# The feed-forward runs of an encoder trunk: the last columns first, then five seven-product groups on a tree of bank copies

## The chip, the core and the metric

The kernel runs on one core of a Trainium2 chip. The metric is the device time of one execution in microseconds (us). The kernel before takes 909.61 us, the median of two timed runs (909.1 and 910.12). Five engines work side by side: TensorE (PE, with PEld its weight loads), VectorE (DVE), ScalarE (ACT), GpSimd (POOL) and SyncE (SP), which issues loads.

## The reference

Two layers; x is 256 tokens of 1024 numbers in float32, and the inner width FF is 2816.

```python
def swiglu(h, w_gate, w_up, w_down):
    return (jax.nn.silu(h @ w_gate) * (h @ w_up)) @ w_down

for l in range(DEPTH):                      # DEPTH = 2
    x = x + 0.5 * swiglu(rms_norm(x, ffn1_norm[l]), ffn1_w_gate[l], ffn1_w_up[l], ffn1_w_down[l])
    h = rms_norm(x, mix_norm[l])
    ...                                     # h @ w_in, windowed and differential attention
    x = x + jnp.concatenate([out_a, out_b], axis=-1) @ w_out[l]
    x = x + 0.5 * swiglu(rms_norm(x, ffn2_norm[l]), ffn2_w_gate[l], ffn2_w_up[l], ffn2_w_down[l])
return rms_norm(x, final_norm)
```

## The kernel before

There are four feed-forward runs, called F1 to F4: layer 0's first (F1) and second (F2), layer 1's first (F3) and second (F4). Between F1 and F2, and between F3 and F4, stand the attention stages; F3 follows F2 directly.

**Precision.** Each weight is loaded as float32 into one of six raw buffers (`N_RAW`), by SP's queue. It is then split in two halves of 128x1024: ScalarE casts the high part (`CAST w<-raw`), VectorE takes the rest as the low part (`TENSOR_TENSOR w<-raw,w`). Activations are split in the same way (`CAST s<-ps`, `TENSOR_TENSOR s<-ps,s`). A product is then three matmuls: high by high, low by high, high by low. A product of a 128-token block with a 512x512 block of weights is 12 matmuls of 512 columns.

**Groups.** The inner width is five groups of 512 columns and a last piece of 256. Of a group, the gate and up weights are four blocks: a and d of the gate (upper and lower half of the 1024 inputs), b and c of the up weight. With two blocks of 128 tokens a group takes eight products of 12 matmuls. Most groups use seven products on sums of blocks, after Strassen and Winograd: sums of activations (`make_sums`, the q and v tiles) against sums of weights. In F1 groups 2 to 4 go by seven, in F2 to F4 groups 1 to 4; the others are plain. A sum of weights is made in a raw buffer, either by VectorE (`plus`, 128x2048) or by a load that POOL issues and that accumulates on arrival (`gather`). The results of several products are combined by accumulating in the same PSUM bank, by copies of banks on ScalarE and by additions on VectorE.

**From hidden to output.** The gated product (`silu` on ScalarE, `up` on VectorE) is turned by TensorE (`turn_one`: four transposes of 128x128; `turn` for the 256-column piece), split, and multiplied with the down weight, whose sums stay in PSUM over the run (`accs`). The last 256 columns (`gu`) come at the end of a run: their down product (`rest`, `tail`) follows group 4's first down product. Then `ffn_close` adds the result to x (`Residual.add`, `xk<-xk,ps`), and starts the next stage's norm: x is turned (`nxt.pair`), evicted with the gain and split, and its squares are summed.

**Order.** `Kept` (line 62 is where every instruction is issued, so all have one line in the profile) holds ScalarE, VectorE and POOL in the order of the program in the feed-forward runs; TensorE always. So an instruction that waits holds up all that stands behind it on its engine. The weights form one list of steps (`specs`). `ahead(n)` issues loads, sums (`prep`) and splits up to half step n. The tables in `LEAD` say, call by call of `go()`, how many half steps ahead of the current product that goes.

## Time and profile before

| | before |
|---|---|
| median of two runs | 909.61 us |
| span of the profiled execution | 907.5 us |
| PE busy | 899.1 us (99%) |
| DVE busy | 785.9 us (87%) |
| ACT busy | 609.8 us (67%) |
| POOL busy | 63.2 us (7%) |
| bytes by DMA | 200.83 MB, 221 GB/s |
| TensorE clock granted | 9 tenths or more in each of 40 slices |

The profiled execution has a span of 907.5 us; no total of its own is listed, and the timed runs' median is 2.1 us above its span, which is taken as what lies around a span. A row of the timeline reads: start, duration, engine, line, operation, output and inputs, count, and in brackets the idle time before it with what ended that. Neighbouring instructions of one form are one row with a count; other engines' rows lie in between. A row of the groups reads: busy time and mean ns of one, then idle time ahead and its releaser.

### The profile page before, as it was taken

The numbers are of one execution on the slowest core, as the hardware profiler recorded it, in microseconds if no ns is written. First come the engines' busy times: TensorE is split into PE (matmuls) and PEld (weight loads), VectorE is DVE, ScalarE is ACT, GpSimd is POOL, SyncE is SP. The second block draws the span as 40 slices with busy tenths as digits, with TensorE's granted clock in tenths as the row PEclk, the third lists the DMA queues.
The fourth block names the chain that finished last, engine by engine and source line by source line (L and its number), as shares of the span: only waits on it lengthen the run. The fifth ranks groups of instructions, "written<-read, shape, count | busy, mean of one in ns | idle before, by whom it ended". The sixth has DMA issues, their size and how long they took to land.

```text
span 907.5 us, 12030 instructions
## 1 busy us (share of the span) xinstructions
PE 899.1 (99%) x4468; PEld 751.0 (83%) x4468; DVE 785.9 (87%) x1069; ACT 609.8 (67%) x970; POOL 63.2 (7%) x79
## 2 busy tenths in 40 slices
PE   9999999999999999999999999999999999999997
PEld 7888888888888888888888888888888888888886
DVE  5968999879987899999778999988888978999894
ACT  6946677666776776677575776667667785776660
POOL 0401000000001001000000001000000000101011
PEclk9999999999999999999999999999999999999999
DMA  9998897954148798897976898899611786898731
GB/s 328 355 287 213 236 309 247 268 143 179 47 150 241 174 265 247 247 300 256 279 204 171 250 278 258 252 303 248 182 57 48 263 223 166 234 312 255 219 114 47
DMA packets 114331, 200.83 MB, mean 221 GB/s; under 512 B 3678, under 2 KB 31648, under 8 KB 114272
## 3 DMA queue, kind: packets, MB, share of 16 engines
q1 hardware_dynamic: 97616, 167.66, 54.4%
q0 software_dynamic: 16096, 31.75, 20.1%
q8 instruction: 35, 0.57, 0.2%
q10 hardware_dynamic: 560, 0.66, 0.2%
q14 instruction: 24, 0.20, 0.1%
HBM read 199.00 MB, written 1.05 MB: 220 GB/s over the span
## 4 chain that ended last, share of the span: by engine, by line
PE 98%; DMA 1%; issue 0%; SPq 0%; DVE 0%; POOLq 0%; POOL 0%
PE ps L62 73%; PE xy L62 25%; DMA xk<-in_x_dram 1%; SPq L172 0%; DVE s L62 0%; DVE xk L62 0%; POOLq L1285 0%; POOL rf L62 0%; SPq L469 0%; SPq L465 0%; DVE tot L62 0%; DVE tmp L62 0%
## 5 line engine op out<-in xcount | busy, mean ns | idle before, releaser
L62 DVE TENSOR_TENSOR w<-raw,w 128x1024 fp32r<-128x1024 f32 (+1 forms) x458 | 476.4, 1097 | 34.6 <-ACT w L62 33.2
L62 PE MATMUL ps<-w,s 128*128 128x512 f32 (+1 forms) x2046 | 473.6, 389 | 0.0
L62 PEld LDWEIGHTS ps<-w,s 128*128 128x128 f32 x2046 | 379.9, 188 | 78.7 <-issue 0.8
L62 ACT CAST w<-raw 128x1024 fp32r<-128x1024 f32 (+1 forms) x457 | 403.9, 954 | 54.0 <-DVE raw L62 38.7
L62 PE MATMUL xy<-w,s 128*128 128x512 f32 x528 | 125.8, 392 | 0.0
L62 PEld LDWEIGHTS xy<-w,s 128*128 128x128 f32 x528 | 98.2, 188 | 20.4
L62 PE MATMUL xy<-w,q 128*128 128x512 f32 x360 | 88.1, 393 | 0.0
L62 PEld LDWEIGHTS xy<-w,q 128*128 128x128 f32 x360 | 66.5, 188 | 13.3
L62 PE MATMUL ps<-s,w 128*128 128x512 f32 (+1 forms) x384 | 69.8, 338 | 0.0
L62 DVE TENSOR_TENSOR raw<-raw,raw 128x2048 f32<-128x2048 f32 x30 | 68.6, 2288 | 0.5
L62 POOL DMA_DIRECT2D raw<-in_ffn_w_up_dram x30 | 38.9, 1313 | 430.1 <-DVE w L62 264.9
L62 PEld LDWEIGHTS ps<-s,w 128*128 128x128 f32 x384 | 58.6, 188 | 8.5
L62 ACT ACTIVATE s<-ps,gcol 128x256 fp32r<-128x256 f32 (+1 forms) x80 | 31.4, 479 | 34.0 <-PE ps L62 34.0
L62 ACT CAST s<-ps 128x512 fp32r<-128x512 f32 x36 | 20.4, 592 | 43.2 <-PE ps L62 43.0
L62 PE MATMUL ps<-w,q 128*128 128x512 f32 x180 | 43.2, 389 | 0.0
L62 PE MATMUL ps<-w,v 128*128 128x512 f32 x180 | 43.2, 389 | 0.0
L62 DVE TENSOR_TENSOR s<-ps,s 128x512 fp32r<-128x512 f32 x36 | 24.1, 686 | 19.5 <-ACT s L62 19.3
L62 PEld LDWEIGHTS ps<-w,v 128*128 128x128 f32 x180 | 33.8, 188 | 7.0
L62 PEld LDWEIGHTS ps<-w,q 128*128 128x128 f32 x180 | 33.8, 188 | 7.0
L62 ACT ACTIVATE s<-s,negm 128x256 f32<-128x256 f32 x64 | 31.8, 498 | 5.3 <-DVE negm L62 5.3
L62 ACT COPY ps<-ps 128x512 f32<-128x512 f32 x15 | 8.6, 570 | 34.4 <-PE ps L62 34.4
L62 DVE SCALAR_TENSOR_TENSOR s<-ps,gcol,s 128x256 fp32r<-128x256 f32 x48 | 20.3, 477 | 13.0 <-ACT s L62 12.9
(131 smaller groups left out, 584.3 us busy)
## 6 DMA issues: line engine op xcount, KB each, us to landing
raw<-in_ffn_w_down_dram SPq DMA_DIRECT2D x44, 1024.0 KB, 7.0
raw<-in_ffn_w_gate_dram SPq DMA_DIRECT2D x39, 1024.0 KB, 7.7
raw<-in_ffn_w_up_dram SPq DMA_DIRECT2D x39, 1024.0 KB, 7.1
raw<-in_ffn_w_up_dram POOLq DMA_DIRECT2D x30, 1024.0 KB, 10.0
raw<-in_w_in_dram SPq DMA_DIRECT2D x14, 1024.0 KB, 6.7
raw<-in_ffn_w_gate_dram SPq DMA_DIRECT2D x8, 512.0 KB, 7.9
raw<-in_ffn_w_up_dram SPq DMA_DIRECT2D x8, 512.0 KB, 8.9
raw<-in_w_in_dram SPq DMA_DIRECT2D x8, 512.0 KB, 6.0
```

Source lines behind the costliest of these rows:

```text
L62: ins = issue(*a, **k)
```

## The change

In F2, F3 and F4 (`run`, `run_on`, `run_close` in place of the old loop):

- The last 256 columns come first: their first half (`g0`), then product a of group 0, then their second half (`g4`). Their hidden piece is turned after product d, and `rest` multiplies it at once. `rest` for the second half of the outputs comes in group 1.
- Group 0 also goes by seven, so all five groups do.
- The seven products accumulate in another order (`by_seven`): four banks A, B, Q, Y, where a is copied from A to Q, abc goes on in A and is copied to Y, and so on, with one copy more and one addition fewer.
- In group 0 (`WAYS`: "cd") both sums abc and abcd are made by accumulating loads of POOL. Block c is now loaded for itself (`load_also`).
- New tables of leads for each run, and another order of sums in `make_sums`, whose signs use `nhr`, the negated `hr`.
- At a run's end the down products of group 3 and 4 remain, with group 4's turn between; the residual of the second half is added by the next run (`late`, `late_sums`).

F1's groups 2 to 4 use the new `by_seven` too. In all, the list of instructions has 30 matmuls of 512 columns and 12 of 256 fewer, 18 weight splits and casts more, and 12 accumulating loads more (30 to 42).

**TensorE at the turn of the last 256 columns' hidden piece.** Before, at the end of F2: `s_807` is the hidden piece, `s_804` the turned halves of group 4, `ps_3058` and `ps_3225` banks of the output.

```order
L62 MATMUL ps_3059<-w_3997,s_804_4077 128x512 x2
L62 MATMUL ps_3059<-w_3998,s_804_4077 128x512
L62 MATMUL ps_4140<-ident,s_807_4108 128x128 x4
L62 MATMUL ps_3058<-w_3997,s_804_4077 128x512 x2
L62 MATMUL ps_3058<-w_3998,s_804_4077 128x512
L62 MATMUL ps_3059<-w_3997,s_804_4077 128x512 x2
L62 MATMUL ps_3059<-w_3998,s_804_4077 128x512
L62 MATMUL ps_3225<-w_4027,s_802_4069 128x512 x2
L62 MATMUL ps_3225<-w_4028,s_802_4069 128x512
L62 MATMUL ps_3226<-w_4027,s_802_4069 128x512 x2
L62 MATMUL ps_3226<-w_4028,s_802_4069 128x512
L62 MATMUL ps_3058<-w_4001,s_815_4145 128x512 x2
```

After, in F2's head: `xy_2806` is bank Q with the last matmuls of product d, `s_551` the hidden piece, `s_560` the same turned and split.

```order
L78 MATMUL xy_2806<-w_2743,s_527_2821 128x512
L78 MATMUL xy_2806<-w_2742,s_527_2821 128x512 x2
L78 MATMUL xy_2806<-w_2743,s_527_2821 128x512
L78 MATMUL ps_2874<-ident,s_551_2924 128x128 x4
L78 MATMUL ps_2983<-w_2835,s_560_2959 128x512 x2
L78 MATMUL ps_2983<-w_2836,s_560_2959 128x512
L78 MATMUL ps_2984<-w_2835,s_560_2959 128x512 x2
L78 MATMUL ps_2984<-w_2836,s_560_2959 128x512
```

The turn had twelve matmuls of other work behind it, six of them into `ps_3058` and six into `ps_3225`; now the turned piece is used by the matmul that follows.

**ScalarE at the same place.** Before: `tmp_4104` and `tmp_4106` are the silus of the last 256 columns, `s_815` the cast of the turned piece.

```order
L62 CAST s_802_4069<-ps_4064 128x2x256
L62 CAST s_804_4077<-ps_4072 128x2x256
L62 ACTIVATE tmp_4104<-xy_4021,r_2890 128x256
L62 ACTIVATE tmp_4106<-xy_4022,r_2890 128x256
L62 CAST w_4112<-raw_3929 128x1024
L62 CAST w_4116<-raw_3929 128x1024
L62 CAST s_815_4145<-ps_4140 128x2x256
L62 CAST w_4154<-raw_3969 128x1024
```

After: `tmp_2920` and `tmp_2922` are the silus of the last 256 columns, `tmp_2953` the silu of product d (`g0`), `s_560` the cast of the turned piece.

```order
L78 COPY xy_2806<-ps_2873 128x512
L78 CAST w_2914<-raw_2668 128x1024
L78 ACTIVATE tmp_2920<-ps_2790,r_2851 128x256
L78 ACTIVATE tmp_2922<-ps_2791,r_2851 128x256
L78 CAST w_2927<-raw_2670 128x1024
L78 CAST w_2931<-raw_2670 128x1024
L78 CAST w_2935<-raw_2003 128x1024
L78 ACTIVATE tmp_2953<-xy_2806,r_2851 128x512
L78 CAST s_560_2959<-ps_2874 128x2x256
L78 CAST w_2962<-raw_2003 128x1024
L78 CAST q_2970<-tmp_2967 128x4x128
```

Two weight casts stood between the silus and the cast of the turned piece; now three casts and a 512-column silu do. VectorE has its splits in the same order.

**VectorE at the head of F3.** Before: `xk` with `ps_3225` and `ps_3226` are the additions of the second half of the residual, ahead of the turn of x's second half.

```order
L62 TENSOR_TENSOR w_4215<-raw_4035,w_4214 128x1024
L62 SCALAR_TENSOR_TENSOR s_833_4229<-ps_4224,gcol,s_833_4229 128x256 x2
L62 SCALAR_TENSOR_TENSOR s_835_4239<-ps_4234,gcol,s_835_4239 128x256 x2
L62 TENSOR_TENSOR xk<-xk,ps_3225 128x512
L62 TENSOR_TENSOR xk<-xk,ps_3226 128x512
L62 TENSOR_TENSOR w_4267<-raw_4035,w_4266 128x1024
L62 SCALAR_TENSOR_TENSOR s_845_4299<-ps_4294,gcol,s_845_4299 128x256 x2
```

After, the same place: `ps_3121` and `ps_3122` are the banks of that half.

```order
L78 TENSOR_TENSOR w_4211<-raw_4049,w_4210 128x1024
L78 SCALAR_TENSOR_TENSOR s_819_4220<-ps_4215,gcol,s_819_4220 128x256 x2
L78 SCALAR_TENSOR_TENSOR s_821_4230<-ps_4225,gcol,s_821_4230 128x256 x2
L78 TENSOR_TENSOR w_4257<-raw_4044,w_4256 128x1024
L78 TENSOR_TENSOR xk<-xk,ps_3121 128x512
L78 TENSOR_TENSOR xk<-xk,ps_3122 128x512
L78 SCALAR_TENSOR_TENSOR s_833_4285<-xy_4279,gcol,s_833_4285 128x256 x2
L78 SCALAR_TENSOR_TENSOR s_834_4294<-xy_4280,gcol,s_834_4294 128x256 x2
```

A weight split (`w_4257`) now stands ahead of the two additions, where they had followed the low parts of the first half directly.

**ScalarE at the end of F2**, after the change only: `tmp_4079` is the silu of product abcd of group 4, `s_803` and `s_804` the casts of the turned hidden group 4.

```order
L78 ACTIVATE tmp_4079<-xy_2806,r_2851 128x512
L78 CAST w_4081<-raw_3856 128x1024
L78 CAST w_4086<-raw_3856 128x1024
L78 CAST w_4090<-raw_3977 128x1024
L78 CAST w_4094<-raw_3977 128x1024
L78 CAST w_4098<-raw_4010 128x1024
L78 CAST w_4124<-raw_4010 128x1024
L78 CAST s_803_4134<-ps_2874 128x512
L78 CAST s_804_4141<-xy_2807 128x512
```

Six weight casts stand between the silu and the first of the two casts.

The diff, cut to its core (`also`, `taker`, the old functions taken out and the unchanged parts are left out):

```diff
-SEVEN = ((2, 3, 4), (1, 2, 3, 4))
+SEVEN = (2, 3, 4)
+ORDER = (("g0", "a", "g4", "d", "ab", "rest", "bc", "abc", "c", "abcd"),
+         ("a", "d", "dn0", "ab", "abc", "bc", "c", "abcd"),
+         ("a", "dn1", "d", "dn0", "ab", "abc", "bc", "c", "abcd"))
+WAYS = ("cd", "", "", "", "")
...
+            head1=(2, 5, 10, 10, 10, 10, 10, 11, 14, 14, 14, 14, 15, 15, 15, 16, 16, 17, 21, 21, 22, 22, 22, 22, 22, 23),
+            end1=(6, 7, 12, 12, 13, 14),
...
+        parts = dict(a=Step(4, 512, load(a), key=a, free=[]),
+                     d=Step(4, 512, load(d), key=d, free=[]),
+                     ab=Step(4, 512, None, src=a, free=[], also=(c, w[c])),
+                     abc=Step(4, 512, None, prep=plus(c, a), src=a, free=[]),
+                     bc=Step(4, 512, load(b), key=b, added=True),
+                     c=Step(4, 512, None, src=c, added=False),
+                     abcd=Step(4, 512, None, prep=plus(d, a), src=a, free=[a, d], early=2))
+        steps = [parts[o] if isinstance(o, str) else o for o in order]
+        def begin():
+            if b in raws:
+                issue(gather(c, b), 1)
+            else:
+                parts["bc"].behind = gather(c, b)
+
+        steps[steps.index(parts["a"]) + 1].prep = lambda: issue(gather(b, a), 1)
+        steps[steps.index(parts["d"]) + 1].prep = begin
+        if "c" in ways:
+            parts["abc"].prep = None
+            steps[steps.index(parts["ab"]) + 1].prep = lambda: issue(gather(c, a), 1)
+        if "d" in ways:
+            parts["d"].free, parts["abcd"].free = [d], [a]
+            parts["abcd"].prep = None
+            steps[steps.index(parts["abc"]) + 1].prep = lambda: issue(gather(d, a), 1)
+        return steps
...
+        def run_specs(wg, wu, wd):
+            down = lambda g, h: plain(wd[l], h * 512, 512, 4 * g, 4)
+
+            def gu(k0):
+                def moves(t, ws=(wg[l], wu[l])):
+                    return [(t[:, :, h * 256:h * 256 + 256], rows(w, FF - 256, 256, k0, 4)) for h, w in enumerate(ws)]
+                return Step(4, 512, moves)
+
+            rest = plain(wd[l], 0, D, 4 * NGRP, 2)
+            for g in range(NGRP):
+                what = dict(g0=lambda: gu(0), g4=lambda: gu(4), rest=lambda: rest,
+                            dn1=lambda: down(g - 2, 1), dn0=lambda: down(g - 1, 0))
+                order = [what[o]() if o in what else o for o in ORDER[min(g, 2)]]
+                specs.extend(seven(wg[l], wu[l], g * 512, order, WAYS[g]))
+            specs.extend((down(NGRP - 2, 1), down(NGRP - 1, 0), down(NGRP - 1, 1)))
+
+        if l:
+            run_specs(g1, u1, d1)
...
+            s1 = add(b1, t1)
             high(s1)
             yield
-            low(0, v)
-            s2 = add(t0, s1, ALU.subtract)
-            low(1, s1)
-            b0_ = add(b0, s2, ALU.subtract)
-            yield
-            high(b0_)
+            s2 = less(s1, t0)
+            low(0, s1)
             high(s2)
             yield
-            low(2, b0_)
-            low(3, s2)
+            low(1, s2)
+            yield
+            v = add(t0, t1)
+            high(v)
+            yield
+            b0_ = less(s2, b0)
+            low(2, v)
+            high(b0_)
+            yield
+            low(3, b0_)
...
+        def late_sums(self, k, into=None):
+
+            if k == 1:
+                for j in range(2):
+                    self.nxt.pair(2 + j, into[j])
+            elif k == 2:
+                self.squares(1)
+                self.nxt.stats()
+                flush()
+
...
+        def by_seven(banks, take, go, then):
+
+            A, B, Q, Y = banks
+            prod(norm.quarter(0, 0), take("a"), A, True)
+            act.copy(Q, A)
+            then("a")
+            prod(norm.quarter(0, 1), take("d"), Q)
+            g0 = silu(flat(), Q, 0)
+            go()
+            then("d")
+            prod(norm.summed(1), take("abc"), A)
+            act.copy(Y, A)
+            go()
+            prod(norm.summed(0), take("ab"), B, True)
+            e = flat()
+            act.copy(e, B)
+            go()
+            then("abc")
+            prod(norm.summed(2), take("bc"), A)
+            act.copy(Q, A)
+            u1 = flat()
+            dve.tensor_tensor(u1, A, e, op=ALU.add)
+            go()
+            then("bc")
+            prod(norm.summed(3), take("c"), Y)
+            u0 = flat()
+            dve.tensor_tensor(u0, Y, e, op=ALU.add)
+            h = blk(F32)
+            up(h, u0, g0, 0, norm.nhr)
+            go()
+            prod(norm.quarter(1, 1), take("abcd"), Q)
+            g1 = silu(flat(), Q, 1)
+            go()
+            up(h, u1, g1, 1, norm.nhr)
+            return h
+
+        def run():
+
+            take = taker(ORDER[0])
+            caps, places = [iter(LEAD[t + str(which)]) for t in ("head", "aux")]
...
+            aux = counted()
+            go()
+            gu = [bank(), bank()]
+            w = take("g0")
+            tokens(gu, norm.xs, w, 0, (0, 1))
+            xy = pair()
+            norm.late(1, xy)
+            go()
+            tokens(gu, norm.xs, w, 0, (2, 3))
+            due(1)
+            hE, wr = [], []
+
+            def rest(h=0):
+                if not wr:
+                    wr.append(take("rest"))
+                accs.append([bank(), bank()])
+                tokens(accs[h], [None] * (2 * NGRP) + hE, wr[0], 4 * NGRP, range(2), first=4 * NGRP, last=-1, h=h)
+
+            banks = bank(), bank(), *xy
+
+            def then(what):
+                if what == "a":
+                    go()
+                    tokens(gu, norm.xs, take("g4"), 4)
+                    go()
+                    due(2)
+                    hE.append(hidden(gate([b[:, 0:256] for b in gu]), [b[:, 256:512] for b in gu]))
+                    go()
+                elif what == "d":
+                    hE[:] = turn(hE[0], 1, [banks[1]])
+                    go()
+                    rest()
+                    go()
+                    due(5)
+                elif what == "abc":
+                    due(7)
+                elif what == "bc":
+                    due(8)
+
+            return run_on(by_seven(banks, take, go, then), banks, rest)
+
+        def run_on(h, banks, rest, old=None, groups=range(1, NGRP)):
+            upto, more = [0], [None]
+
+            def go(table=None):
...
+            for g in groups:
+                go("next" if g == 1 else "last" if g == groups[-1] else "more")
+                new = []
+                take = taker(ORDER[min(g, 2)])
+                if aside is not None and rest is not None and g == groups[-1]:
+                    aside()
+
+                def then(what):
+                    if what == "a":
+                        if g > 1:
+                            add(old, g - 2, 1, take("dn1"))
+                        else:
+                            rest(1)
+                        go()
+                        new.append(turn_one(h, 0, banks[1]))
+                        go()
+                        new.append(turn_one(h, 1, banks[3]))
+                        go()
+                    elif what == "d":
+                        add(by_token(new), g - 1, 0, take("dn0"))
+                        go()
+
+                h = by_seven(banks, take, go, then)
+                old = by_token(new)
+            if rest is None:
+                return h, old
+            take = lambda: weights(99, True)
+            go("end")
+            w = take()
+            add(old, NGRP - 2, 1, w, range(3))
+            go()
+            new = by_token([turn_one(h, 0, banks[1]), turn_one(h, 1, banks[3])])
+            add(old, NGRP - 2, 1, w, range(3, 4), last=(-1, G4 - 1 if which == 2 * LAYERS - 1 else -1))
+            return accs, new, take, go
+
...
+    def run_close(parts, nxt):
+        accs, new, take, go = parts
+        res = Residual(nxt, accs)
+        go()
+        w = take()
+        tokens(accs[0], new, w, G4, first=-1, last=G4 + 3)
+        for t in range(2):
+            res.add(0, t)
+        go()
+        w = take()
+        tokens(accs[1], new, w, G4, (0, 1), first=-1, last=G4 + 3)
+        go()
+        for j in range(2):
+            nxt.pair(j)
+        nxt.copies(2)
+        res.squares(0)
+        tokens(accs[1], new, w, G4, (2, 3), first=-1, last=G4 + 3)
+        go()
+        for t in range(2):
+            res.add(1, t)
+        nxt.late = res.late_sums if nxt.sums else res.late
 
...
         nxt_norm.pair(0)
         out_part(w, 6, 1, [(0, 1)])
         nxt_norm.pair(1)
+        nxt_norm.copies(2)
+        res.squares(0)
         out_part(w, 6, 1, [(1, 1)])
-        res.squares(0)
         for t in range(2):
             res.add(1, t)
-        nxt_norm.late = res.late
+        nxt_norm.late = res.late_sums
```

324 lines of the change are left out of this document (151 added, 173 removed).

## The prediction

> **What bounds the kernel now.** I read the page's busy times and its chain of waits first, then the busy time by stage, then TensorE's own timeline.
>
> ```profile
> span 907.5 us, 12030 instructions
> PE 899.1 (99%) x4468; PEld 751.0 (83%) x4468; DVE 785.9 (87%) x1069; ACT 609.8 (67%) x970; POOL 63.2 (7%) x79
> PE 98%; DMA 1%; issue 0%; SPq 0%; DVE 0%; POOLq 0%; POOL 0%
> 277.69:306.19 28.50, 28.50 (x139) 23.81 (x138) 21.75 (x32) 21.76 (x41) 2.71 (x3) 1.00 0.84 222
> 337.04:367.85 30.81, 30.81 (x143) 25.60 (x141) 29.50 (x28) 21.90 (x27) 2.57 (x2) 1.00 0.90 257
> 425.97:452.30 26.33, 26.33 (x126) 21.89 (x125) 21.12 (x23) 17.09 (x21) 1.31 (x1) 1.00 0.93 284
> ```
>
> TensorE is busy 99% of the span and 98% of the chain of waits is TensorE itself: whatever else is done today is hidden. The three stretches (columns: length, then busy time of PE, PEld, DVE, ACT and POOL, the clock, the DMA share, GB/s) are the head of the second feed-forward run, its steady group 3, and its end. TensorE never waits in any of them. But in the steady group VectorE has only 30.81 − 29.50 = 1.31 us to spare; in the head 6.75, at the end 5.21. So two things count: how many matmuls go, and whether the work around the new places of use still comes in time. The later runs are called F2, F3, F4 here, as in the description of the kernel.
>
> ```profile
> 309.04 8.32 PE L62 MATMUL ps<-w,s 128*128 128x512 f32 x36
> 317.20 1.07 PE L62 MATMUL ps<-w,q 128*128 128x512 f32 x4
> L62 PE MATMUL ps<-w,s 128*128 128x256 f32 x36 | 4.5, 283 | 0.0
> ```
>
> The pace is (317.20 − 309.04)/36 = 0.2267 us for a 512-column matmul, so 2.72 for a product of 12, and 4.5/36 = 0.125 for 256 columns.
>
> **Part 1, the matmuls.** Group 0 goes from eight products to seven in three runs; the instruction lists hold 30 fewer 512-column matmuls and 12 fewer of 256. 30 × 0.2267 + 12 × 0.125 = 8.3 us less. All of TensorE's time is on the path, so this counts in full: **−8.3**.
>
> **Part 2, the hidden piece of the last 256 columns.** Before, it was turned at the end of the run:
>
> ```profile
> 441.85 0.60 PE L62 MATMUL ps<-ident,s 128*128 128x128 f32 x4
> 442.20 6.19 PE L62 MATMUL ps<-w,s 128*128 128x512 f32 x26
> 442.48 0.59 ACT L62 CAST s<-ps 128x512 fp32r<-128x512 f32 x1 [2.14 <-PE ps L62]
> 443.10 0.69 DVE L62 TENSOR_TENSOR s<-ps,s 128x512 fp32r<-128x512 f32 x1 [1.31 <-ACT s L62]
> ```
>
> The four transposes take 442.20 − 441.85 = 0.35, ScalarE sees them 0.28 later, and both halves are ready at 443.79, 1.59 after the turn. TensorE had 12 other matmuls (2.72 us) to do meanwhile. Now `rest` follows the turn at once, and its second matmul pair needs the low half 0.227 later: even on empty queues that is a stall of 1.59 − 0.227 = 1.36, or 4.1 in three runs. That is a floor which no table of leads can move. But the queues are not empty, as the ScalarE order shows: two silus, two to four weight casts and the silu of `g0` stand ahead of the cast, and VectorE keeps the same order.
>
> ```profile
> 437.62 0.84 ACT L62 ACTIVATE tmp<-xy,r 128x256 f32<-128x256 f32 x2 [4.43 <-PE xy L62]
> 438.13 0.88 DVE L62 SCALAR_TENSOR_TENSOR s<-xy,hr,tmp 128x256 f32<-128x256 f32 x2 [2.34 <-ACT tmp L62]
> 424.36 7.68 ACT L62 CAST w<-raw 128x1024 fp32r<-128x1024 f32 x8
> 425.42 9.17 DVE L62 TENSOR_TENSOR w<-raw,w 128x1024 fp32r<-128x1024 f32 x8
> 299.92 1.27 ACT L62 ACTIVATE tmp<-ps,r 128x512 f32<-128x512 f32 x2
> ```
>
> Prices: a cast 7.68/8 = 0.96; a split (9.17 − 1.22)/7 = 1.136 in a row, where 1.22 is one that waits; a 512-column silu 0.64. Let E be the end of the second half of the last 256 columns (`g4`). TensorE does product d (2.72) and the turn (0.35): `rest` starts at E+3.07, and the low half is due at E+3.30. F2: ScalarE's silus from E+0.28 to 1.12, three casts to 4.00, silu to 4.64, cast of the hidden piece to 5.23; VectorE's two multiplications to 1.67, three splits from about 2.2 (behind the first cast) to 5.6, low half to 6.3: 3.0 late. F3, two casts: splits to 4.5, low half 5.2: 1.9 late. F4, four casts: splits to 6.75, low half 7.4: 4.1 late. Sum **+9.0**; bounds 4.1 (the floor) and 13 (each another 1.3 late, were a cast behind a load).
>
> **Part 3, the residual at F3's head.** VectorE's order now has a split ahead of the two additions to `xk` that the second transposes need.
>
> ```profile
> 285.41 1.03 PE L62 MATMUL ps<-ident,xk 128*128 128x128 f32 x8
> 286.05 1.57 ACT L62 ACTIVATE s<-ps,gcol 128x256 fp32r<-128x256 f32 x4 [2.44 <-PE ps L62]
> 286.20 3.00 PE L62 MATMUL ps<-w,s 128*128 128x512 f32 x12
> 287.49 0.65 ACT L62 ACTIVATE junk<-xk 128x512 f32<-128x512 f32 x1
> 288.88 3.00 ACT L62 ACTIVATE s<-ps,gcol 128x256 f32<-128x256 f32 x8
> 281.17 1.27 DVE L62 TENSOR_TENSOR xk<-xk,ps 128x512 f32<-128x512 f32 x2
> ```
>
> From the first transposes: TensorE takes 0.79 (285.41 to 286.20) and 24 matmuls (5.44), so the second transposes are due at 6.23. ScalarE: visible at 0.64, four evictions 1.57, four more 1.50, two squares with their readings 1.4 (287.49 to 288.88), then the cast 0.96 to 6.1; VectorE: split to 7.2, two additions 1.27 to 8.5. That is **+2.2**, bounds 0 (the cast done before the squares have to be) and 3.2.
>
> **Part 4, the end of F2.** Its table of leads puts six casts between the silu of `g1` and the cast of the turned hidden group; before, the steady groups had up to four at such a place, with more products behind them. From the end Z of product abcd: visible 0.28, silu 0.64, six casts 5.76, to Z+6.7; the last split to 7.9, the low half to 8.6. TensorE has 18 matmuls, eight transposes (0.79) and six matmuls: due at Z+6.46 with the second matmul. **+2.1**, bounds 0 and 3.
>
> **Part 5, the sums of weights of group 0.** Two of them are now made by accumulating loads that POOL issues, not by VectorE.
>
> ```profile
> raw<-in_ffn_w_up_dram SPq DMA_DIRECT2D x39, 1024.0 KB, 7.1
> raw<-in_ffn_w_up_dram POOLq DMA_DIRECT2D x30, 1024.0 KB, 10.0
> L62 POOL DMA_DIRECT2D raw<-in_ffn_w_up_dram x30 | 38.9, 1313 | 430.1 <-DVE w L62 264.9
> L62 ACT COPY ps<-ps 128x512 f32<-128x512 f32 x15 | 8.6, 570 | 34.4 <-PE ps L62 34.4
> DMA packets 114331, 200.83 MB, mean 221 GB/s; under 512 B 3678, under 2 KB 31648, under 8 KB 114272
> ```
>
> In F2 the load that makes abcd can only be issued when abc's buffer has been split, at about E+7.5 (6.3 and one split). It lands 10.0 later, at 17.5; four casts (3.84) and then the copy of product bc (0.57, the row `COPY ps<-ps`) end at 21.9, since that copy stands behind those casts on ScalarE. TensorE wants to go on into that bank at E + 3.07 + 3.0 + 5 × 2.72 = 19.7. **+2.2**; bounds 0 (a landing in 7.1, as SP's) and 6 over the three heads. F3 and F4, where the copy stands ahead of more of the casts, I put at 0 within these bounds.
>
> The Trainium skill ("DMA: Bandwidth & Descriptors", section "Anatomy of one DMA — SWDGE (gpsimd) path") gives such a load about 2.0 us plus its bytes over 436e3, an estimate of 4.4 us for 1 MB. The trace's 10.0 speaks against it at this DMA load; by the rule part 5 would be 0 and the time 2.2 lower.
>
> **What is put at nothing.** 18 more splits (20.4 us on VectorE) and casts (17.3 on ScalarE), 6 of each a run: 6 × 1.136 = 6.8 against 6.75 + 5.21 idle in head and end; uncovered it is that 6.8 a run, the case D below. The new tree in F1's groups 2 to 4: one copy (0.57) more on an engine busy 67%, one VectorE addition fewer. SP issues as many loads as before. Places where the order leaves only some 0.1 to 0.5 us (the low halves of abc, the split ahead of F3's last residual) I take at 0, since the stalls above give their engines the time; bounds 0 and 4.
>
> **The sum.** −8.3 + 9.0 + 2.2 + 2.1 + 2.2 = +7.2: a span of 907.5 + 7.2 = 914.7. The median of the two timed runs is 909.61, 2.1 above the span; with that, **916.8 us**. All lower bounds together: −8.3 + 4.1 = −4.2, 905.4. All upper ones: −8.3 + 13 + 3.2 + 3 + 6 + 4 = +20.9, 930.5.
>
> **The rivals.**
> A, the sum above: the tight places each show as a wait of TensorE. 0.58.
> B, only the floor of part 2 is paid: the casts and splits that stand ahead run earlier than my chains have them, because the loads and buffers let the leading products' splits drain in the head's idle VectorE time (6.75 us). 905.4; were the turn free too, 909.6 − 8.3 = 901.3. For it: no stage of before shows a wait. Against it: the casts stand behind the silus in the queue, and a queue is not overtaken. 0.24.
> C, slower: the accumulating loads decide. Four of them stand one behind another in POOL's queue in each head, three of them ahead of `r` (the normalisation's power, on which every silu waits), while the DMA share is already 0.84 to 0.93. If one takes 15 us instead of 10, each head's abcd is 5 us later: 916.8 + 15 = 931.8. It decides above about 13.7 us (11/3 more than now). For it: 10.0 is already 2.9 more than SP's loads; against it: POOL's are 30 of before's loads, and 12 more are 12.6 MB on 200. 0.13.
> D, VectorE becomes the bound in every group: 1.31 us of slack, and a tree with more tight orders; 1 us more in 15 groups is 931.8 too. Against it: a steady group has one addition less. 0.05.
>
> The Trainium skill ("SBUF — State Buffer", section "SBUF: two separate sides") warns that VectorE's two-port operations lock POOL out of writing descriptors, which would speak for C. The trace shows no sign: POOL's issues take 1313 ns on average though VectorE is busy 87% of the span, so C has no more from it.
>
> **Range and chances.** What a measurement here tells from no change is about 2%, from 891.4 to 927.8. Range 903 to 927: it holds A but for its upper tail, and B but for the free turn, together some 0.8. Slower by over 2% is C and D less their milder halves, and A's tail: 0.12. Faster by 2% would take 18 us where only 8.3 are removed: 0.01. The same: 0.87.
>
> **What the new profile would show.** TensorE's busy time 8 to 9 us lower and a busy share of some 97 to 98%. A gap of 1.4 to 4 us right behind each lone group of four transposes of the heads (part 2); with B each is 1.4. A gap ahead of the second `xk` transposes of F3 (part 3), one behind the eight transposes at F2's end (part 4), one in F2's head ahead of abcd with ScalarE's copy as releaser (part 5). With C the POOL loads' median from issue to landing is above 13 us; with D gaps of about 1 us in every group, with VectorE's splits as releaser. Wrong I would be if these gaps are absent, or if the largest lies elsewhere.

## The result

The changed kernel takes **955.07 us** (median of two runs, 953.35 to 956.79) against 909.61: a ratio of 1.0504, interval 1.0483 to 1.0525. It is 5% slower, and 38 us beyond the forecast of 916.8; the range ended at 927.

The page of the changed kernel, its span, engines, chain of waits and accumulating loads:

```profile
span 955.0 us, 11983 instructions
PE 917.3 (96%) x4426; PEld 746.8 (78%) x4426; DVE 807.3 (85%) x1082; ACT 635.1 (67%) x1002; POOL 76.6 (8%) x91
PE 55%; DVE 17%; DMA 12%; issue 9%; ACT 6%; POOLq 0%; POOL 0%; SPq 0%; DVEq 0%; ACTq 0%
raw<-in_ffn_w_up_dram POOLq DMA_DIRECT2D x39, 1024.0 KB, 11.6
```

TensorE was 98% of the chain of waits and is 55% now. VectorE (17%), loads (12%) and ScalarE (6%) hold most of the rest; 9% are "issue", time in which the engine waited for nothing that the profile shows. TensorE's busy time rose by 18 us with fewer matmuls, partly because some ran at half clock and many at a slower pace (below).

To see where, I took each stretch between two turns of a hidden group and subtracted its ideal: matmuls by 0.2267 us and transposes by 0.0985 (0.79/8). Before, every such stretch of the feed-forward runs is 0.1 to 0.4 us above it. Now, in us above the ideal:

| stretch | F1 | F2 | F3 | F4 |
|---|---|---|---|---|
| head (turn of the last columns to the turn of group 0) | | 4.05 | 1.98 | 6.24 |
| the three stretches behind it, group by group | 1.00, 2.33, 2.59 | 1.86, 1.29, 5.58 | 0.86, 1.36, 1.35 | 2.62, 2.14, 2.45 |
| the last group, to its turn | | 0.83 | 1.30 | 3.86 |
| the run's end and the next head | | 10.05 | 1.85 | 0.14 |

(F3's 1.85 is what the stretch from its end through the projections grew by, beyond four more transposes; the ideal of their 256-column matmuls isn't known as well.) Together 55.7. Less what before had in such stretches (about 2.4) and the 8.3 of the matmuls, plus a start that was 1.2 us later in this execution, that is 46, of 47.5 that the span grew. So the matmuls did go, and some 55 us came in their place. By the starts of all matmuls, this is of three kinds, each against before:

- 41 us are gaps of over 0.1 us in which TensorE waits.
- 6.5 us are matmuls at half clock.
- 6.8 us are a slower pace at full clock. In each of the 18 groups by seven, some 45 matmuls from product abc on start 0.231 and 0.236 us apart by turns, not 0.2267. Neither before nor the kernel of the last experiment, whose waits go up to over 7 us, has such a run of matmuls. Why the new order has them, no run here shows.

Five stretches of the changed kernel (columns as in the prediction): the heads of F2 and F4, F2's last-but-one stretch, F2's end with F3's head, and a steady group of F3.

```profile
304.25:330.45 26.20, 23.51 (x101) 18.26 (x100) 22.12 (x25) 17.59 (x23) 3.92 (x3) 1.00 0.91 231
775.46:803.86 28.40, 24.69 (x101) 19.59 (x100) 22.19 (x24) 17.21 (x22) 3.92 (x3) 0.94 0.83 212
395.04:431.33 36.29, 33.58 (x141) 26.51 (x140) 29.38 (x27) 21.83 (x26) 2.57 (x2) 0.95 0.85 235
458.79:499.77 40.98, 35.54 (x151) 28.52 (x150) 29.06 (x38) 27.17 (x46) 4.56 (x4) 0.92 0.95 258
555.48:587.55 32.07, 31.55 (x141) 25.40 (x140) 29.13 (x27) 21.95 (x27) 2.57 (x2) 1.00 0.91 260
```

The steady group has VectorE busy for 29.13 us, less than the 29.50 of before in 30.81, and yet it takes 32.07. So the sum of VectorE's work alone doesn't explain it, and the order is suspected. VectorE's and ScalarE's way to this group's product abc:

```profile
550.22 0.57 ACT L78 COPY xy<-ps 128x512 f32<-128x512 f32 x1 [2.08 <-PE ps L78]
550.70 4.85 ACT L78 CAST w<-raw 128x1024 fp32r<-128x1024 f32 x5
551.78 5.77 DVE L78 TENSOR_TENSOR w<-raw,w 128x1024 fp32r<-128x1024 f32 x5 [1.86 <-ACT w L78]
558.67 2.35 DVE L78 TENSOR_TENSOR w<-raw,w 128x1024 fp32r<-128x1024 f32 x2
561.05 2.29 DVE L78 TENSOR_TENSOR raw<-raw,raw 128x2048 f32<-128x2048 f32 x1
563.38 2.00 ACT L78 CAST w<-raw 128x1024 fp32r<-128x1024 f32 x2 [3.40 <-DVE raw L78]
564.46 2.36 DVE L78 TENSOR_TENSOR w<-raw,w 128x1024 fp32r<-128x1024 f32 x2 [1.12 <-ACT w L78]
565.74 0.51 PE L78 MATMUL ps<-w,q 128*128 128x512 f32 x1 [0.53 <-DVE w L78]
```

The copy of product a waits for TensorE; five casts stand behind it on ScalarE, and VectorE idles 1.86 us for them. From there it works without a long pause through seven splits and the turned group to the addition for abc (561.05), and abc's split comes late. Abc starts 14.3 us after the copy (564.53), stops after two matmuls, and the next group's copy of a, which comes behind it on TensorE, starts at 582.28, 32.06 us after this one. That is a loop, and idle time outside it can't shorten it.

### The profile page after: what moved, and what is told of

The parts are those of the page before. It is cut to its first block, busy times and chain, and to the rows that moved or that the text cites. A ratio compares the mean times of both kernels' runs of the same rounds, so it can differ in the third digit from the quotient of the medians.

```text
span 955.0 us, 11983 instructions
## 1 busy us (share of the span) xinstructions
PE 917.3 (96%) x4426; PEld 746.8 (78%) x4426; DVE 807.3 (85%) x1082; ACT 635.1 (67%) x1002; POOL 76.6 (8%) x91
## 4 chain that ended last, share of the span: by engine, by line
PE 55%; DVE 17%; DMA 12%; issue 9%; ACT 6%; POOLq 0%; POOL 0%; SPq 0%; DVEq 0%; ACTq 0%
PE ps L78 40%; PE xy L78 15%; DMA raw<-in_ffn_w_up_dram 12%; DVE w L78 11%; ACT w L78 4%; DVE raw L78 4%; DVE s L78 1%; ACT s L78 1%; DVE xk L78 1%; ACT junk L78 0%; DVE tmp L78 0%; DMA raw<-in_ffn_w_gate_dram 0%; ACT tmp L78 0%; ACT xy L78 0%; POOLq L1474 0%
## 5 line engine op out<-in xcount | busy, mean ns | idle before, releaser
L78 PE MATMUL ps<-w,s 128*128 128x512 f32 (+1 forms) x1716 | 408.6, 394 | 12.5 <-ACT s L78 6.5
L78 PEld LDWEIGHTS ps<-w,s 128*128 128x128 f32 x1716 | 321.6, 190 | 84.9 <-ACT s L78 8.3
L78 PE MATMUL ps<-w,q 128*128 128x512 f32 x648 | 160.9, 402 | 11.4 <-ACT w L78 5.4
L78 PE MATMUL xy<-w,s 128*128 128x512 f32 x672 | 164.6, 395 | 2.7 <-ACT xy L78 2.7
L78 PEld LDWEIGHTS ps<-w,q 128*128 128x128 f32 x648 | 120.8, 190 | 49.3 <-DVE w L78 12.6
L78 PEld LDWEIGHTS xy<-w,s 128*128 128x128 f32 x672 | 124.2, 189 | 30.3 <-ACT xy L78 4.2
L78 PE MATMUL xy<-w,v 128*128 128x512 f32 x216 | 53.3, 395 | 0.0
L78 ACT COPY xy<-ps 128x512 f32<-128x512 f32 x54 | 31.2, 578 | 26.9 <-PE ps L78 26.6
L78 PEld LDWEIGHTS xy<-w,v 128*128 128x128 f32 x216 | 40.6, 188 | 9.8
L78 PE MATMUL ps<-ident,s 128*128 128x128 f32 x216 | 28.7, 272 | 0.0
## 6 DMA issues: line engine op xcount, KB each, us to landing
raw<-in_ffn_w_up_dram POOLq DMA_DIRECT2D x39, 1024.0 KB, 11.6
```

What stands on the lines that cost most here:

```text
L78: ins = issue(*a, **k)
```

## The experiments

Theory 1 is this order on VectorE (and ScalarE). Theory 2: the accumulating loads land late. Theory 3: VectorE has too much to do. Kernels that shorten an operation leave out a part of its work.

**Product ab ahead of abc.**

```diff
-            prod(norm.summed(1), take("abc"), A)
-            act.copy(Y, A)
-            go()
             prod(norm.summed(0), take("ab"), B, True)
             e = flat()
             act.copy(e, B)
             go()
+            prod(norm.summed(1), take("abc"), A)
+            act.copy(Y, A)
+            go()
```

> The changed kernel with product ab ahead of product abc on TensorE, in every group by seven; nothing else. Theory 1 (the order): in a steady group abc is wanted right behind the first down product, but its sum is made by VectorE behind the splits of ab and is split itself after that, and VectorE gets to it late, because the casts stand behind the copy of product a on ScalarE. Twelve other matmuls (2.72 us) in between are more than the 0.9 to 2.3 us that the groups lose, so the steady groups of the three later runs go back to about 30.8 us from 31.6 to 33.3, and the run takes 930 to 938 us. Theory 2 (the loads): the accumulating loads land late; whoever needs them waits as before, 950 to 956. Theory 3 (VectorE has too much to do in a group): the wait moves to the next product, 950 to 956.

Measured 1009.12 us, ratio 1.1099 (1.1073 to 1.1126): 54 slower than the changed kernel, which none of the three expected. A steady group of F3:

```profile
562.04 2.28 DVE L78 TENSOR_TENSOR raw<-raw,raw 128x2048 f32<-128x2048 f32 x1
564.36 1.99 ACT L78 CAST w<-raw 128x1024 fp32r<-128x1024 f32 x2 [2.23 <-DVE raw L78]
566.25 0.58 ACT L78 COPY xy<-ps 128x512 f32<-128x512 f32 x1
566.88 4.49 PE L78 MATMUL ps<-w,q 128*128 128x512 f32 x12 [4.21 <-ACT xy L78]
```

Bank A must be copied into Y before bc goes on in A. Product ab, into another bank, had covered that copy. Without it TensorE waits 4.21 us, since the copy stands behind two casts, and these behind VectorE's addition. The edit tested its own mistake more than the theory; it shows what ab is there for.

**A short addition, short loads, and both.**

```diff
-abc=Step(4, 512, None, prep=plus(c, a), src=a, free=[])
+abc=Step(4, 512, None, prep=plus(c, a, slice(0, 1)), src=a, free=[])   # a quarter of the columns
...
-pool.dma_start(raws[to], w[k], accum_op=ALU.add)
+pool.dma_start(raws[to][:, small], w[k][:, small], accum_op=ALU.add)   # a quarter, groups 1 to 4
```

> The changed kernel in which VectorE's addition for abc does only a quarter of its columns (128x512, about 0.7 us, where it was 128x2048, 2.29), so the sum is not complete; order and loads stay. Theory 1 (the order on VectorE): abc is ready 1.6 us earlier, and the waits of 0.9 to 1.4 us a group in the later runs go, those of 2 to 2.6 shrink: 934 to 942 us. Theory 2 (the loads): within 3 us of 955. Theory 3 (VectorE's sum of work): 1.6 us less in each of 15 groups brings the groups back as well, 932 to 940; then the groups with ab first stay slow.

> The changed kernel in which the accumulating loads of groups 1 to 4 bring a quarter of their bytes (256 KB of 1 MB), so the sums are not complete; group 0's stay. Theory 1 (the order): only the one wait that ends with a load goes, that of F2's last group (about 5 us with what follows from it); 946 to 953 us. Theory 2 (the loads): the groups go back to 30.8 us, 925 to 935 us.

> The short addition for abc (a quarter of its columns) and the short accumulating loads of groups 1 to 4 (a quarter of the bytes) together; the sums are not complete. Alone they took 16.8 and 13.6 us off. If the groups' waits are two layers, one by VectorE's order and one by the loads, each seen only where the other is shorter, both together take off the whole of the groups' 29 us but for 0.5 us a group: 930 to 934 us, with the groups at 30.7 to 31.3. If a third thing holds the groups, 936 to 941.

Measured 938.24, 941.43 and 933.82 us. Short loads leave F3's steady groups as they were, and take off most of what F1, F2's third stretch and F4 had above 1.3; with the short addition too, all come to about 0.4 to 1.0. F1's second stretch by seven and one of F3, first F1's as changed (F3's is above), then both with short loads, then with short loads and the short addition:

```profile
98.55:131.60 33.05, 31.80 (x142) 25.39 (x141) 29.28 (x28) 21.86 (x26) 2.57 (x2) 1.00 0.90 255
```
```profile
98.68:130.32 31.64, 31.55 (x141) 25.39 (x140) 29.18 (x28) 21.81 (x26) 1.73 (x2) 1.00 0.69 217
546.28:578.38 32.10, 31.57 (x141) 25.39 (x140) 29.05 (x27) 21.94 (x27) 1.72 (x2) 1.00 0.68 213
```
```profile
97.41:128.68 31.27, 31.27 (x141) 25.54 (x140) 27.51 (x28) 21.84 (x26) 1.73 (x2) 1.00 0.70 223
545.68:576.92 31.24, 31.24 (x141) 25.55 (x140) 27.33 (x27) 21.90 (x27) 1.72 (x2) 1.00 0.65 216
```

F3's group stays at 32.1 with short loads and falls to 31.24 with the short addition. F1's falls from 33.05 to 31.64 with the loads and to 31.27 with both. But how late loads come differs from execution to execution: two later experiments, which leave F1 as changed and its loads whole, have the same stretch at 31.63 and 34.41 (the end of F2, and short casts and splits):

```profile
97.98:129.61 31.63, 31.53 (x141) 25.39 (x140) 29.17 (x28) 21.82 (x26) 2.57 (x2) 1.00 0.92 267
```
```profile
97.54:131.95 34.41, 32.10 (x142) 25.31 (x140) 29.30 (x28) 21.85 (x26) 2.57 (x2) 1.00 0.85 243
```

So F1's stretch alone shows nothing about the loads; the medians, and the groups taken together, do. There are two layers. With short loads, nearly every group still loses 0.8 to 1.4 us, of which about 0.5 is mostly the slower pace and stays with both short. Where the loads are late, they cost up to 4 us more. The two hide each other, so the gains (16.8, 13.6) don't add: both give 21.3. With both short, the gaps of over 0.1 us in the 15 groups fall from 22.2 us in all to 1.7, so hardly any wait is left there. The short addition alone can't tell theory 1 from 3, since it also makes VectorE's work less; the next experiment changes the order alone.

**Product ab ahead, but covered.** Six matmuls of the first down product are put behind abc.

```diff
+                left = then("d")                  # dn0 without its last six matmuls
+                w_ab, w_abc = take("ab"), take("abc")
+                prod(norm.summed(0), w_ab, B, True)
+                ...
+                prod(norm.summed(1), w_abc, A)
+                act.copy(Y, A)
+                go()
+                left()
```

> The changed kernel in which, in groups 1 to 4, product ab goes ahead of abc, the weights of abc are issued before ab, and the last six matmuls of the first down product go behind abc, where they cover the copy of bank A into Y. So abc starts 1.36 us later than in the changed kernel, and no copy is waited for. If VectorE's order sets the waits of 0.9 to 1.4 us in every steady group, they go where no load is late (F3's groups at 30.7 to 30.9 us, from 31.6 to 32.1), and about 12 us in all: 940 to 946 us. If the wait is for VectorE's sum of work, it moves to the next product: 953 to 957. If the copy of bank A is still late, as with ab first and nothing behind abc, slower than 960.

Measured 949.91 us (ratio 1.0445, 1.0429 to 1.046). F3's first steady stretch goes to 31.25, from 31.58, and its second to 31.67, from 32.07, with all of VectorE's work left in. But its third goes to 32.46, from 32.06: there casts wait 1.74 and 0.58 us for loads, which they don't in the first.

```profile
588.16 2.00 ACT L78 CAST w<-raw 128x1024 fp32r<-128x1024 f32 x2 [1.74 <-DMA raw<-in_ffn_w_up_dram]
```

A gain of 5 where 12 were expected: the groups together lose 24.9 us for 31.4. Where no load is late the order's wait goes, which supports theory 1; elsewhere a load's takes its place.

**The end of F2.**

```diff
-            end1=(6, 7, 12, 12, 13, 14),
+            end1=(3, 3, 10, 12, 13, 13),
```

> The changed kernel with another table for the end of F2, (3, 3, 10, 12, 13, 13) for (6, 7, 12, 12, 13, 14): two casts instead of six stand between the silu of the last product and the cast of the turned hidden group, and no split stands ahead of the second two additions to xk at F3's head. By parts 3 and 4 of the prediction both waits go (the trace of the changed kernel has 3.9 and 2.4 us there); and if it is the two waits that bring the two stretches of half clock behind them (3.4 us each), those go with them, 1.7 us each: 945 to 947 us in all. If the splits are only wanted a little later and hold up something else: 950 to 955, with a new wait within F3's head. If the half clock has another cause: 948.5 to 950.

Measured 951.19 us (948.3 to 955.3). The two waits went (that stretch is 2.48 above its ideal, from 10.05), but F3's head rose from 1.98 to 9.02:

```profile
493.26 1.99 ACT L78 CAST w<-raw 128x1024 fp32r<-128x1024 f32 x2 [4.01 <-DMA raw<-in_ffn_w_up_dram]
495.74 0.57 ACT L78 CAST s<-ps 128x512 fp32r<-128x512 f32 x1
496.37 0.79 PE L78 MATMUL ps<-w,s 128*128 128x512 f32 x1 [5.01 <-ACT s L78]
```

A cast ahead of the turned piece's waits 4.01 us for a load. That splits put off free their raw buffers later, and loads so start later, would explain it; that step was not tried by itself.

**The turned piece's cast first.**

```diff
-            head1=(2, 5, 10, 10, 10, 10, 10, 11, 14, 14, 14, 14, 15, 15, 15,
+            head1=(2, 5, 10, 10, 10, 10, 10, 11, 12, 12, 12, 12, 15, 15, 15,
-            head3=(0, 2, 4, 10, 10, 10, 10, 10, 14, 14, 14, 14, 14, 15, 15, 15,
+            head3=(0, 2, 4, 10, 10, 10, 10, 10, 11, 11, 11, 11, 15, 15, 15, 15,
```

> The changed kernel with one or no weight cast between the silus of the last 256 columns and the cast of the turned piece, in the heads of F2 and F4 (the tables head1 and head3 hold back 12 and 11 there instead of 14, and give 15 behind the turn). By part 2 of the prediction the waits behind the turn shrink from 3.0 and 4.1 us to about 1.5 each, near the floor of 1.36, and with F4's the half clock behind it (1.7 us) goes: 949 to 951 us. If the casts that were put off are wanted at once by the next product, the wait moves there, within the head: 953 to 957.

Measured 953.94 us, no gain. F2's head (6.34 above its ideal, from 4.05):

```profile
301.28 0.50 PE L78 MATMUL ps<-w,s 128*128 128x512 f32 x1 [0.82 <-ACT s L78]
302.00 2.81 PE L78 MATMUL ps<-w,s 128*128 128x512 f32 x11 [0.22 <-DVE s L78]
307.00 0.51 PE L78 MATMUL ps<-w,q 128*128 128x512 f32 x1 [2.20 <-ACT q L78]
307.73 4.44 PE L78 MATMUL ps<-w,q 128*128 128x512 f32 x12 [0.22 <-DVE q L78]
```

Behind the turn 0.82 + 0.22 us are left, but product abc now waits 2.20 + 0.22 for its sum of activations, and its matmuls start at half clock. The wait moved by one product, as the second expectation said.

**What the heads are short of.** Three kernels halve the weights' low parts (VectorE), the high parts (ScalarE) or both, in group 0 and in the last three down products. A fourth gives group 0's sums to VectorE. Two more add the short addition and the short loads: one to the halved low parts, the other to both halves, with group 0's loads short too.

```diff
+            if i in short:                                    # short splits; short casts: the same for the cast
+                r_, h_, l_ = [t[:, 0:1] for t in (r_, h_, l_)]
             dve.tensor_tensor(l_, r_, f(h_), op=ALU.subtract)
...
-WAYS = ("cd", "", "", "", "")
+WAYS = ("", "", "", "", "")                                   # additions by VectorE
```

> The changed kernel in which VectorE makes only half of each low weight part (128x512 for 128x1024, 0.57 for 1.14 us or so), in group 0 and in the last three down products of F2, F3 and F4; the products use that half twice, so the results aren't complete. ScalarE's casts, the loads and the order stay. Theory: heads and ends lose their 23 us (with the half clock in them) because VectorE has too much to do there in too tight an order; then 13 of these go, 936 to 944 us, with the heads at 1 to 2.5 us of excess each and the stretch from F2's end to F3's at under 4. Rival, ScalarE's order (its casts stand ahead of what is waited for): within 4 us of 955, and the next kernel is the one that gains.

> The same for the other engine: ScalarE casts only half of each high weight part in the same steps (128x512 for 128x1024, 0.5 for 0.96 us), used twice; VectorE's splits keep their size. Theory VectorE: within 4 us of 955, since each split starts where VectorE is free, not where the cast ends. Theory ScalarE: 936 to 944 us. Where both queues stand ahead of the same wait by turns: 945 to 951 each.

> The changed kernel with both of group 0's sums made by VectorE's additions (2.29 us each) instead of POOL's accumulating loads, as in the other groups. If VectorE is what the heads are short of, 1 to 5 us more in each: 958 to 970 us. If the accumulating loads of the heads are what is waited for there (the rival C of the prediction, and its part 5), faster: 945 to 952 us.

> The short addition, the short loads and the short splits together. If the account is right, what is left over the ideal of 901 us (909.6 less the 8.3 of the matmuls) is the floor of part 2 (4.1), some 0.5 us in each of 15 groups (7.5), and a few us in F2's end: 913 to 919 us. If something else holds heads or ends: above 922.

> The changed kernel with casts and splits of weights both halved in group 0 and in the last three down products of F2, F3 and F4 (half of each part, used twice); loads and groups 1 to 4 stay. If the two queues hold heads and ends by turns: heads at 1.4 to 2 us of excess, the stretch from F2's end at under 4, 936 to 941 us. If the accumulating load of abc is the third that takes its turn: the heads of F2 and F4 stay at 3 to 5 us, 942 to 947, and the wait behind the turn begins with a cast that waits for a load.

> The same, with all accumulating loads at a quarter of their bytes, group 0's too, and the short addition for abc. If loads, VectorE and ScalarE are all that is late, 901 (the ideal) + 4 to 6 in the heads (the floor of part 2 is 4.1) + some 7 in the groups + 3 to 4 at F2's end: 915 to 919 us. If the heads still lose 4 us or more each with a half clock: 922 to 927, and the cause is in the order of the dependences, not in any size.

Measured: short splits 948.46, short casts 949.78, both 941.79; additions by VectorE 968.16; everything but the casts and group 0's loads short 929.31 (913 to 919 was expected, so that account missed something); everything short 918.35. Splits and casts alone both lie in the 945 to 951 expected where the two queues hold the heads by turns. The three heads lose 5.13, 2.03 and 5.61 us with short splits, 2.84, 2.11 and 5.52 with short casts, and 2.14, 2.01 and 2.68 with both, whose 941.79 us lies between the two outcomes expected. In F2's head with both engines short, the piece behind the silus still waits in a queue:

```profile
303.29 0.62 ACT L78 CAST w<-raw 128x512 fp32r<-128x512 f32 x1 [0.82 <-DMA raw<-in_ffn_w_up_dram]
304.40 0.57 ACT L78 CAST s<-ps 128x512 fp32r<-128x512 f32 x1
305.03 0.50 PE L78 MATMUL ps<-w,s 128*128 128x512 f32 x1 [0.94 <-ACT s L78]
```

So ScalarE's casts and VectorE's splits hold the heads of F2 and F4 by turns. The accumulating load for abc comes third, and is a small part: with all short, heads are 1.98, 1.99 and 2.07 above the ideal. F2's end goes from 5.35 with short casts and splits to 1.91. With additions in place of those loads the three heads cost 4.4, 3.1 and 5.4 us more, so the loads were the better way here. F2's head, its end and a group of F3 with all short:

```profile
299.10:323.24 24.14, 23.10 (x101) 18.46 (x100) 16.90 (x23) 14.23 (x21) 2.67 (x3) 1.00 0.64 181
444.87:477.71 32.84, 31.78 (x152) 26.03 (x151) 19.02 (x37) 18.68 (x43) 3.81 (x5) 1.00 0.77 253
533.09:564.32 31.23, 31.23 (x142) 25.55 (x141) 27.32 (x27) 21.88 (x27) 1.73 (x2) 1.00 0.67 212
```

The 918.35 lies in the 915 to 919 expected for "loads, VectorE and ScalarE are all that is late". It is still over 909.4. The gaps of over 0.1 us are 8.7 us more than before's there, so even with all this work cut short, waits take back the 8.3 us that the change saves. Another 7 us are the slower pace, which this kernel shows without any wait:

```profile
536.72 5.60 PE L78 MATMUL ps<-w,s 128*128 128x512 f32 x24
542.16 8.56 PE L78 MATMUL ps<-w,q 128*128 128x512 f32 x36
550.56 2.96 PE L78 MATMUL xy<-w,v 128*128 128x512 f32 x12
```

The 24 matmuls of the down product start (542.16 − 536.72)/24 = 0.2267 us apart, the 36 behind them (550.56 − 542.16)/36 = 0.2333.

**The half clock.** The changed kernel's record of the granted clock has four stretches at half speed inside the work, 3.41 us each, all behind a wait. One in F4's head, in windows of 3.41 us:

```profile
777.23:780.64 3.41, 0.87 (x3) 0.51 (x4) 3.29 (x5) 3.05 (x4) 0.00 (x0) 1.00 0.97 311
780.64:784.05 3.41, 3.41 (x10) 2.63 (x9) 3.33 (x5) 1.23 (x2) 1.32 (x1) 0.50 0.87 309
784.05:787.46 3.41, 3.41 (x16) 2.78 (x15) 0.09 (x1) 0.00 (x0) 0.00 (x0) 1.00 1.03 165
```

To test it apart from this kernel, waits of growing length were put into the kernel before:

```diff
+            if t == 0:
+                for _ in range(LADDER[rung[0]]):     # 0, 4, 5, 0, 6, 7, 8, 0, 9, 10, 11, 0, 12, 14, 16
+                    act.copy(hb[:, 0], sl)
             act.copy(hb[:, 0], sl)
```

> The kernel before, which has no wait of TensorE, with 4 to 16 more copies (0.57 us each) on ScalarE ahead of the cast of the turned hidden group, in eleven of its groups, so that TensorE waits there for a growing time. Theory of the window: the granted clock is halved for 3.41 us behind any 3.41 us of a free-running grid in which TensorE was idle for more than some 1.35 to 1.65 us; so rungs with a wait below 1.3 us show none, and nearly all with more than 2 us show one, at 1.7 us of time each. Rival, the clock only falls behind a whole idle window: no rung with a wait below 3.41 us shows it. The Trainium skill ("TensorE: Matmul & The Clock Gate", section "Part 1: The HAM clock gate (the "warmup" mystery)") states the rival: half rate after at least one idle window of about 3.4 us. Second rival: the half clock of the changed kernel has to do with something else in it, and this kernel shows none.

Measured 964.25 us in one run, against 909.59. Two rungs, one with waits of 2.62 and 0.5 us that two windows share about evenly, one of 3.22:

```profile
406.58:409.99 3.41, 1.98 (x9) 1.31 (x7) 0.07 (x1) 3.22 (x7) 0.00 (x0) 1.00 1.08 372
409.99:413.40 3.41, 2.15 (x8) 1.56 (x9) 2.25 (x3) 3.38 (x6) 0.00 (x0) 1.00 1.07 338
526.04:529.45 3.41, 0.35 (x2) 0.19 (x1) 0.34 (x1) 3.28 (x6) 0.00 (x0) 1.00 0.79 298
529.45:532.86 3.41, 3.22 (x8) 2.42 (x8) 3.27 (x5) 3.41 (x5) 1.29 (x1) 0.50 0.03 9
```

All six rungs whose waits are 3.22 us or longer brought half clock, and none of the five with 2.62 or less. So it is no property of the changed kernel: a wait does it, if enough of it falls into one window. My bound (1.35 to 1.65 us) was too low; the section on the hardware has the one that all traces give. The rival of a whole idle window falls with the window of F4's head shown above, in which TensorE was busy for 0.87 us, and with many like it.

## Why the prediction was wrong

- **Part 1, the matmuls (−8.3): the count right, the pace not.** The 8.3 us went, but some 45 matmuls in each of 18 groups start 0.231 to 0.236 us apart, not 0.2267 as the part takes them all to do. That gives back 6.8 us, a term that the prediction doesn't have.
- **Part 2, the turned piece: right.** Foretold 3.0, 1.9 and 4.1 us. TensorE's waits behind the turn are 1.73 + 0.87, 0.82 + 0.23 and 3.35 + 0.36 us. A bracket counts only from the end of the last matmul, and the part counts against the pace; from start to start, less 0.2267, it is 3.05, 1.49 and 4.16: 8.7 for 9.0. In F4 one of the casts ahead waited 0.4 us for a load besides, so there the close fit is in part luck. The floor, foretold as 1.36, is 1.49 counted so where the casts were moved away, and the head then had no better place for them.

```profile
306.58 0.49 PE L78 MATMUL ps<-w,s 128*128 128x512 f32 x1 [1.73 <-ACT s L78]
779.41 0.50 PE L78 MATMUL ps<-w,s 128*128 128x512 f32 x1 [3.35 <-ACT s L78]
```

- **Part 3, the residual: right.** 1.76 + 0.27 us, from start to start 2.4, for 2.2.
- **Part 4, F2's end: right in mechanism, too small.** 0.60 + 2.81 us, from start to start 3.9, for 2.1; the upper bound was 3.

```profile
461.81 0.49 PE L78 MATMUL ps<-w,s 128*128 128x512 f32 x1 [0.60 <-ACT s L78]
465.12 1.20 PE L78 MATMUL ps<-w,s 128*128 128x512 f32 x4 [2.81 <-DVE s L78]
483.10 0.33 PE L78 MATMUL xy<-ident,xk 128*128 128x128 f32 x1 [1.76 <-DVE xk L78]
```

- **Part 5, the copy behind the casts (+2.2): the chain is there, its wait is not.** In F2's head the load for abcd lands after 8.4 us, not 10.0, and the copy behind its casts ends at 322.10. TensorE goes on into that bank at 322.15, 0.1 us late. Of the two loads it is the other one, for abc, that held up the turned piece: by the 0.4 us in F4.

```profile
317.72 3.90 ACT L78 CAST w<-raw 128x1024 fp32r<-128x1024 f32 x4 [0.35 <-DMA raw<-in_ffn_w_gate_dram]
321.52 0.58 ACT L78 COPY xy<-ps 128x512 f32<-128x512 f32 x1
```

- **"What is put at nothing": the step that failed.** I set idle time of VectorE (6.75 + 5.21 us) against 6.8 of new splits, and small margins in the steady groups at 0, bounds 0 and 4. The 15 groups cost 31 us above their ideal, about 30 more than before: 22.2 us of waits, 1.6 of half clock, and the rest mostly pace. It was the error of summing work where the order decides: the steady group's VectorE has less to do than before and still comes late. D named the place and the sign, VectorE's splits as releaser, at 1 us a group and a chance of 0.05; the group's fewer additions, which I held against it, were no argument. The claim that the stalls in the heads would give the engines time was wrong too: F3's three later stretches lose 1.36, 1.35 and 1.30 us one after another, so the lateness comes anew in each.
- **Rival C, the loads: half right.** Their median from issue to landing is 11.6 us (10.0 before), under the 13 that was its sign. The short loads took 13.6 us off, from F1's and F4's groups and F2's third stretch above all, not 5 from each head's abcd.
- **Not in the prediction at all: the half clock**, four stretches, 6.5 us in all. No row of before could show it, since behind the first 15 us no matmul there starts over 0.2 us late.

## What to carry to other kernels

Where engines run in program order, cost a new order by the loop that returns to itself (product, copy, casts, splits, sum, product), not by each engine's busy share: a group of 30.8 us became one of 32.1 with less work on VectorE (29.13 us for 29.50). Cheap tests are kernels in which one operation does a quarter of its work; but take two or three such layers together, since each hides the next. A wait on TensorE costs more than its length once it fills some 2 of the 3.41 us of a clock window. And a new order can change the pace of the matmuls themselves: compare their starts before and after where nothing waits.

## What the runs showed of the hardware

The granted clock of TensorE is set by windows of 3.41 us on a fixed grid: in each trace that has several, the half-clock stretches inside the work start at whole multiples of 3.413 us from each other (408.58, 466.61, 483.68 and 780.64 us in the changed kernel: 17, 5 and 87 windows apart). Over the traces of the changed kernel and the fourteen experiments I added up TensorE's idle time in each window at full clock (start to start of two matmuls, less 0.2267). 59 windows were followed by one at half clock, and each had 2.0 us or more idle. Of the windows with 0.9 to 1.95 us, 136 in all, none was followed by one; above that, two were not (1.99 and 2.03 us). So a wait of just over 2 us that falls into one window costs up to 1.7 us more (half of 3.41), and the one of 2.62 that two windows share cost nothing more. The Trainium skill ("TensorE: Matmul & The Clock Gate", section "Part 1: The HAM clock gate (the "warmup" mystery)") has the half rate and the window of 3.4 us, but says that it takes at least one idle window; the runs show that a window some 60% idle (2.0 of 3.41 us) is enough.

At full clock, 512-column matmuls ran at two paces: 0.2267 us apart in the kernel before, and 0.231 and 0.236 by turns in the changed kernel's products abc to c. What sets the pace is open.
